# The order of the RWKV scan's instructions on TensorE: from a scheduler's order to a fixed one, with a chunk's small products together and the dense work in one block per chunk

## The chip, the cores and the metric

The kernel runs on one core of a Trainium2 chip. The metric is the device time of one execution in microseconds (us). Three executions of the kernel before took 1273.61, 1274.02 and 1277.94 us; the median is 1274.02 us.

## The reference, cut to what matters

The model is a trunk of four sub-layers on 512 positions of width 1024: a spatial-gating MLP, a ConvFFN, an RWKV-7 time mixer, a second ConvFFN, and a last RMSNorm. All of it is float32. The change touches the time mixer only:

```python
def rwkv7_mixer(h, mu, w_r, w_k, w_v, w_o, ...):
    xx = token_shift(h) - h
    xr, xw, xk, xv, xa, xg = (h + xx * mu[n] for n in range(6))
    r, k, v = xr @ w_r, xk @ w_k, xv @ w_v
    w = -softplus(-(w0 + tanh(xw @ w1) @ w2)) - 0.5
    a = sigmoid(a0 + (xa @ a1) @ a2)
    g = sigmoid(xg @ g1) @ g2
    ...
    # per head of 64: S_t = S_{t-1} diag(w_t) + (S_{t-1} a_t) b_t^T + v_t k_t^T ; y_t = S_t r_t
    y = wkv7_scan(r_h, decay, k_h, v_h, -kk, kk * a_h)
    y = group_norm(y) * ln_w + ln_b
    y = y + sum(r_h * k_h * r_k, -1) * v_h        # the bonus
    return (y * g) @ w_o
```

## The kernel before, in words

**Dense products.** A float32 product is made of three products in the format fp32r: `mm3` (L317, L318, L319) multiplies the high part of the weight with the high and the low part of the activation, and the low part of the weight with the high part of the activation. Activations lie transposed, 128 channels on the partitions and 512 positions along the row, so one such matmul is 128x128 by 128x512. They are most of the kernel's work on TensorE (PE).

**The scan.** The recurrence is computed in chunks of 64 positions: two groups of eight heads (four pairs of two heads) times eight chunks, so 16 chunks one after the other. Within a group a chunk needs the state that the chunk before leaves. In plain words a chunk does this, where each product is eight small float32 matmuls (four pairs times two heads) that a profile shows as x16, because a float32 matmul is run in two passes:

- L1194 writes the PSUM tile `us` from the state tile `vu` and the chunk's operand `st`. VectorE (DVE) copies it to `wt` (L1196). L1198 begins the outputs, PSUM tile `e`, from the same two operands.
- L1207 multiplies `wt` with the inverse `ti` into the other half of `us`. DVE copies one half of the heads into `vu` (L1208), ScalarE (ACT) copies the other half (L1209). In the program ACT's copy waits for DVE's, since both write one tile.
- L1216 multiplies `vu` with `bt` into `us`; DVE adds the decayed state `s0`, which GpSimd (POOL) made in L1203, and so writes the next chunk's `vu` (L1219, two instructions). The last chunk of a group has no such step.
- L1221 adds the second part of the outputs to `e` with 64x64 matmuls; ACT copies `e` into the tile `y` (L1224, two instructions).

So a chunk has two round trips between PE and the other engines: L1194, L1196, L1207, and L1207, L1208, L1209, L1216; and a third one through L1219 to the next chunk's L1194.

**After every second chunk** `finish` normalizes `y`: ACT squares it (L1237), DVE sums the squares (L1240), DVE and POOL raise them to the power -0.5 (L369, L370), DVE multiplies (L1243), PE transposes four times (L1247), DVE multiplies and adds (L1250). In the second group `gate` (dense products, L1104 the last of them) follows after every fourth chunk.

**What else PE does meanwhile.** The dense work of the phase is a generator, `fill`: the projections (with `value`, whose small transposes are L829 and whose bonus is L844), the gates' first product (`gates`, with weights of 128 and of 32 columns), and the output projection (`project`). The inverse of the second group's 64x64 triangles is a generator too (`invert(1)`): 31 steps of two instructions on DVE, and then 32x32 matmuls on PE, in 8 lots of 16 (L1030 and L1033).

**What sets the order.** The program is written in the order of the calls, but the framework's scheduler places each engine's instructions by its own estimate of when each is ready. Before, `weave` advances the generator `scan(g)` by a third of a chunk at a time, and after each third issues dense steps at a rate (RATES) and side steps at another, tied to an instruction already written by `issue_after`; the scheduler then mixes them. The loads of the chunks' operands (L1147 for `st`) are issued one chunk ahead on the DMA queue of SyncE (SP); three buffers hold `st`.

**Arrays.** [...] In this stretch there are dense matmuls (128x128 weights), 128x64 ones (L1194, L1198, L1216), 64x64 ones (L1207, L1221), and 32x32 ones (L1030, L1033). "Array mode" below means that shape.

Of the kernel before, what the change touches and what calls it, by code (L numbers as in the profile page):

```python
# [12 lines left out]
F32 = mybir.dt.float32  # L13
# [131 lines left out]
class Emit:  # L145
    def __init__(self, ctx, tc, A, out):
# [37 lines left out]
        self.wq = nc.scalar  # L184
        self.ktiles = 2
        self.x = []

# [112 lines left out]
    def gate_parts(self):  # L300

        t = [self.wp.tile([P, 1024], F32, tag="w32", bufs=2, name=self.uid("w32")) for _ in range(2)]
        for i in range(2):
            self.wq.dma_start(t[i], self.gd[:, i, 0:1024])
        return (1024, [tuple(x.bitcast(F32R) for x in t)]), (512, [self.pair(self.gd[:, :, 1024:], 256)])

# [6 lines left out]
    def mm3(self, acc, w, x, first, last):  # L313

        mm = self.nc.tensor.matmul
        (wh, wl), (xh, xl) = w, x
        mm(acc, wh, xh, start=first, stop=False)  # L317
        mm(acc, wh, xl, start=False, stop=False)  # L318
        mm(acc, wl, xh, start=False, stop=last)  # L319
# [412 lines left out]
    def rwkv_main(self, r, ctx, gain):  # L732
# [90 lines left out]
        def value(m, v):  # L823
# [18 lines left out]
            S.activation(wb, self.c("bones", P), AF.Copy, scale=self.p("r_k", m))  # L842
            q = self.acc("mm")
            nc.tensor.matmul(q, wb, rt[g][:, i, :], start=True, stop=True)  # L844
# [216 lines left out]
        def gates():  # L1061


            ws = ga["parts"]
            accs = [self.acc("mm")[0:n] for n in (P, 32)]
            for k in range(KT):
                x = gx[k]
                if k + 2 < KT:
                    gx.append(gate_mix(k + 2))
                for a, w, n in zip(accs, ws, (P, 32)):  # L1070
                    self.mm3(a, self.wcols(w, k * n, n), x, k == 0, k == KT - 1)
                next(tail[0], None)
                if k >= 3:
                    back(k - 3)
                yield
            for k in range(KT - 3, KT):
                back(k)
            for i, a in enumerate(accs):
                t = scratch("sq")[0:(P, 32)[i]]
                S.activation(t, a, AF.Tanh, scale=0.5)  # L1080
                V.tensor_scalar(t, t, 0.5, 0.5, ALU.mult, ALU.add)
# [83 lines left out]

        left, two = [], []

        def scan(g, late=iter(())):

            ih = [(i, hd) for i in range(4) for hd in range(2)]  # L1170
            y = None

            for c in range(NCH):
                last = c == NCH - 1
# [13 lines left out]

                def pt(i, hd):
                    o = RW * (1 - hd)  # L1190
                    return st[i][H[hd], o:o + C]

                for i, hd in ih:
# [6 lines left out]
                if not last:  # L1200
                    s0 = tile_([P, 4, C], "wt", 4)
                    for hd in range(2):
                        G.tensor_tensor(s0[H[hd]], vu[H[hd], hd], bc(gc[H[hd], 4 * g:4 * g + 4, c], C), ALU.mult)  # L1203
                self.step(late)
                yield
                for i, hd in ih:
                    nc.tensor.matmul(us[H[hd], 1, i, :], ti[g][H[hd], i, c, :], wt[H[hd], i, :], start=True, stop=True)  # L1207
                V.tensor_copy(vu[h0, 0], us[h0, 1])  # L1208
                S.copy(vu[h1, 1], us[h1, 1])  # L1209
                self.step(late)  # L1210
                if g == 1 and c == 0:
                    self.step(late)
                yield
                if not last:
# [3 lines left out]
                    for hd in range(2):  # L1218
                        V.tensor_tensor(nvu[H[hd], hd], us[H[hd], 0], s0[H[hd]], ALU.add)  # L1219
                for i, hd in ih:  # L1220
                    nc.tensor.matmul(e[H[hd], 0, i, :], pt(i, hd), vu[H[hd], hd, i, :],  # L1221
                                     start=False, stop=True, skip_group_check=True)
                for hd in range(2):
                    S.copy(y[H[c % 2], :, hd, :], e[H[hd], 0])  # L1224
                self.step(late)
                yield
                if c % 2 == 1:
                    yield from late
                    late = finish(g, c // 2, y)
            left.append(late)  # L1230

        def finish(g, b, y):
# [4 lines left out]
            S.activation(sq, y3, AF.Square)  # L1237
            yield
            ss, rs = tmp("gs", 2, 8), tmp("gr", 2, 8)
            V.tensor_reduce(ss, sq, AX.X, ALU.add)  # L1240
            self.rsqrt(ep, rs, ss, 1.0 / C, GN_EPS)
            yield
            V.tensor_tensor(y3, y3, bc(rs, C), ALU.mult)  # L1243
            yield
            q = self.acc("aux")
# [7 lines left out]
            if g == 1 and b % 2 == 1:  # L1253
                yield
                while 1 not in gw:
                    next(fill)
                for i in range(4):
                    gate(1, i, slice((b - 1) * P, (b + 1) * P))
                    if i % 2 == 1 and b == 1:
                        yield  # L1260
                if b == 3:
                    gated.add(g)
            yield

# [44 lines left out]
        for _ in inv:  # L1309
            next(fill)  # L1310
            self.step(ahead, (mybir.EngineType.PE,))
        ctx.close()
# [82 lines left out]
```

## Time and profile before

| | |
|---|---|
| median of three executions | 1274.02 us (1273.61 to 1277.94) |
| the profiled execution: its time, its span | 1274.33 us, 1272.5 us |
| mean granted clock of PE | 0.994 |
| PE busy | 1254.8 us, 99% of the span |
| DVE, ACT, POOL busy | 856.5, 629.6, 98.0 us |
| share of PE in the chain that ended last | 90% |
| the scan: first L1194, last L1104 | 737.9 us, 874.1 us |

The span is what the records of the profiled execution cover; its own time holds 1.8 us more. Times inside the execution are counted from the start of the span. A line number is that of the kernel before unless the text says otherwise. In the timelines, x16 is a run of sixteen records of one shape, and the brackets say for how long the engine was idle before it and which instruction it waited for.

### The profile page before, as it was taken

The numbers are of one execution on the slowest core, as the hardware profiler recorded it, in microseconds if no ns is written. First come the engines' busy times: TensorE is split into PE (matmuls) and PEld (weight loads), VectorE is DVE, ScalarE is ACT, GpSimd is POOL, SyncE is SP. The second block draws the span as 40 slices with busy tenths as digits, with TensorE's granted clock in tenths as the row PEclk, the third lists the DMA queues.
The fourth block names the chain that finished last, engine by engine and source line by source line (L and its number), as shares of the span: only waits on it lengthen the run. The fifth ranks groups of instructions, "written<-read, shape, count | busy, mean of one in ns | idle before, by whom it ended". The sixth has DMA issues, their size and how long they took to land.

```text
span 1272.5 us, 19534 instructions
## 1 busy us (share of the span) xinstructions
PE 1254.8 (99%) x7591; PEld 1014.3 (80%) x7591; DVE 856.5 (67%) x1403; ACT 629.6 (49%) x1082; POOL 98.0 (8%) x119
## 2 busy tenths in 40 slices
PE   9999999999999999999999999999999999999997
PEld 6878888888888888887777776677888888888886
DVE  6466568888886444675789887665677777772233
ACT  5534446555555333475686647423544444443232
POOL 4100200000000000000000022222100000000002
PEclk9999999999999999999999999999999999999999
DMA  7332357887556775335878698763233332233332
GB/s 251 108 99 83 123 173 239 244 255 240 198 169 209 216 231 161 105 106 182 220 203 226 202 245 206 203 181 133 83 99 100 100 99 91 94 94 106 93 91 79
DMA packets 115452, 201.65 MB, mean 158 GB/s; under 512 B 21600, under 2 KB 53600, under 8 KB 115360
## 3 DMA queue, kind: packets, MB, share of 16 engines
q10 hardware_dynamic: 39104, 112.87, 29.4%
q1 hardware_dynamic: 76256, 87.54, 23.1%
q8 instruction: 59, 0.97, 0.3%
q14 instruction: 33, 0.27, 0.1%
HBM read 152.93 MB, written 47.45 MB: 157 GB/s over the span
## 4 chain that ended last, share of the span: by engine, by line
PE 90%; DVE 4%; issue 1%; DMA 0%; POOL 0%; ACT 0%; DVEq 0%; ACTq 0%; POOLq 0%
PE mm L317 10%; PE mm L319 9%; PE mm L318 9%; PE aux L317 6%; PE aux L319 6%; PE aux L318 6%; PE e L318 6%; PE e L317 6%; PE e L319 6%; PE us L319 5%; PE us L318 5%; PE us L317 5%; PE aux L935 1%; PE aux L949 1%; PE us L1194 1%; PE e L1221 1%
## 5 line engine op out<-in xcount | busy, mean ns | idle before, releaser
L236 ACT CAST w<-w 128x512 fp32r<-128x512 f32 x340 | 206.8, 611 | 364.6 <-PE aux L319 91.8
L237 DVE TENSOR_TENSOR w<-w,w 128x512 fp32r<-128x512 f32 x340 | 232.1, 685 | 185.2 <-ACT w L236 184.7
L317 PE MATMUL mm<-mxh,w 128*128 128x512 f32 (+1 forms) x416 | 170.5, 410 | 0.0
L318 PE MATMUL mm<-mxl,w 128*128 128x512 f32 (+1 forms) x416 | 164.6, 396 | 0.0
L319 PE MATMUL mm<-mxh,w 128*128 128x512 f32 (+1 forms) x416 | 164.3, 395 | 0.0
L344 POOL TENSOR_TENSOR ss<-ss,sq 128x512 f32<-128x512 f32 x30 | 40.6, 1353 | 771.1 <-issue 592.9
L317 PEld LDWEIGHTS mm<-mxh,w 128*128 128x128 f32 (+1 forms) x416 | 77.6, 187 | 20.0 <-issue 3.3
L319 PEld LDWEIGHTS mm<-mxh,w 128*128 128x128 f32 (+1 forms) x416 | 77.8, 187 | 17.4 <-issue 0.7
L318 PEld LDWEIGHTS mm<-mxl,w 128*128 128x128 f32 (+1 forms) x416 | 77.9, 187 | 16.1 <-issue 1.3
L542 ACT ACTIVATE cv<-z,par 128x512 f32<-128x512 f32 x88 | 71.7, 817 | 28.1 <-DVE z L540 23.1
L317 PE MATMUL aux<-mxh,w 128*128 128x512 f32 x216 | 84.5, 391 | 0.0
L319 PE MATMUL aux<-mxh,w 128*128 128x512 f32 x216 | 84.2, 390 | 0.3 <-DVE w L237 0.3
L317 PE MATMUL us<-mxh,w 128*128 128x512 f32 x216 | 84.5, 391 | 0.0
L318 PE MATMUL aux<-mxl,w 128*128 128x512 f32 x216 | 84.1, 389 | 0.0
L318 PE MATMUL us<-mxl,w 128*128 128x512 f32 x216 | 84.1, 389 | 0.0
L319 PE MATMUL us<-mxh,w 128*128 128x512 f32 x216 | 84.0, 389 | 0.0
L317 PE MATMUL e<-mxh,w 128*128 128x512 f32 x208 | 81.4, 391 | 0.1
L318 PE MATMUL e<-mxl,w 128*128 128x512 f32 x208 | 81.1, 390 | 0.1
L319 PE MATMUL e<-mxh,w 128*128 128x512 f32 x208 | 80.9, 389 | 0.0
L543 DVE SCALAR_TENSOR_TENSOR cv<-z,par,cv 128x512 f32<-128x512 f32 x88 | 66.1, 752 | 20.0 <-ACT cv L542 20.0
L544 DVE SCALAR_TENSOR_TENSOR cv<-z,par,cv 128x512 f32<-128x512 f32 x88 | 66.0, 752 | 2.9
L319 PEld LDWEIGHTS aux<-mxh,w 128*128 128x128 f32 x216 | 40.5, 187 | 9.2 <-DVE w L237 0.8
(1088 smaller groups left out, 2599.0 us busy)
## 6 DMA issues: line engine op xcount, KB each, us to landing
w<-in_wup ACTq DMA_DIRECT2D x88, 512.0 KB, 3.7
w<-in_wdn ACTq DMA_DIRECT2D x32, 512.0 KB, 3.6
st<-std SPq DMA_DIRECT2D x30, 320.0 KB, 6.1
w<-wkd ACTq DMA_DIRECT2D x16, 512.0 KB, 4.8
w<-wvd ACTq DMA_DIRECT2D x16, 512.0 KB, 5.6
w<-wod ACTq DMA_DIRECT2D x16, 512.0 KB, 4.3
w<-in_wdn ACTq DMA_DIRECT2D x16, 384.0 KB, 3.3
w<-in_wsu ACTq DMA_DIRECT2D x8, 512.0 KB, 3.8
```

The source lines that it names most:

```text
L236: nc.scalar.copy(hi[r, :n], src)
L237: (lo_eng or nc.vector).tensor_tensor(lo[r, :n], src, hi[r, :n].bitcast(F32), ALU.subtract)
L317: mm(acc, wh, xh, start=first, stop=False)
L318: mm(acc, wh, xl, start=False, stop=False)
L319: mm(acc, wl, xh, start=False, stop=last)
L344: nc.gpsimd.tensor_tensor(self.ss, self.ss, self.sq, ALU.add)
L542: nc.scalar.activation(c, z[:, 2:], AF.Identity, scale=cw(2, i), bias=self.p("conv_b", l * 44 + i))
L543: nc.vector.scalar_tensor_tensor(c, z[:, 1:T + 1], cw(1, i), c, ALU.mult, ALU.add)
L544: nc.vector.scalar_tensor_tensor(c, z[:, 0:T], cw(0, i), c, ALU.mult, ALU.add)
L935: nc.tensor.matmul(qs[hd][:, c - ch.start, :], bk[H[hd], c, C * hd:C * hd + P], ar[H[hd], c, :], start=True, stop=True)
L949: nc.tensor.matmul(qs[hd][:, c, :], bk[H[hd], c, C * hd:C * hd + P], dg[H[hd], c, :], start=True, stop=True)
L1194: nc.tensor.matmul(us[H[hd], 0, i, :], ar(i, hd, 0), vu[:, hd, i, :], start=True, stop=True)
```

## The change

`scan(0)`, `scan(1)` and the two `weave` calls are replaced by one generator-free loop, `recurrence`, over all 16 chunks, in a section in which PE's instructions stand in the order in which they are written (the other engines' order is still the scheduler's). A chunk is written as: L1235 and L1239 (both 128x64; L1194 and L1198 before), a step of `finish`; L1252 (64x64; L1207 before), the copies to `vu` (L1253, L1254), and then, in the same array mode, the second part of the outputs of the chunk before (`outputs`, L1184; L1221 before) with their copies; L1262 (128x64; L1216 before) and the additions (L1265); those parts of `finish` that need dense matmuls; the 32x32 products of the inverse in the chunks 5, 6 and 7 of the first group (2, 3 and 3 lots); and then one block of dense work, `pump`, of 2.1 us by a count of columns (9 to 12 matmuls). So there is one place per chunk for dense work.

Three smaller edits come with it. `invert(1)` takes up to seven steps for each step of `invert(0)`, which leaves every instruction ahead of the scan where it was. The gates' 32 weight columns are run as 128, the rest zero, which takes a memset of two tiles on POOL (L309). The last value's bonus product takes a PSUM buffer of another tag.

The four listings below are the order of a built program, with no time in it; after the line and the operation stand output and inputs by name (the number behind a name tells buffers apart) and the weights' or the rows' shape.

The first is PE before, from the middle of chunk 3 of the first group to the start of chunk 4, where `e_6839` holds chunk 3's outputs and `us_6945`, `e_6946` belong to chunk 4:

```order
L1221 MATMUL e_6839<-vu_6742,st_6738 64x64
L829 MATMUL mm_6982<-cst,v_6903 128x128 x3
L1216 MATMUL us_6838<-vu_6742,cbt_6741 64x64 x8
L1221 MATMUL e_6839<-vu_6742,st_6738 64x64 x7
L829 MATMUL mm_6982<-cst,v_6903 128x128
L317 MATMUL mm_6905<-mxh_5515,w_1094_6701 128x512
L1194 MATMUL us_6945<-vu_6742,st_6834 64x64
L1198 MATMUL e_6946<-vu_6742,st_6834 64x64
L318 MATMUL mm_6905<-mxl_5516,w_1094_6701 128x512
L1194 MATMUL us_6945<-vu_6742,st_6834 64x64 x7
L1198 MATMUL e_6946<-vu_6742,st_6834 64x64 x7
L1247 MATMUL aux_6968<-cst,y_6656 128x128 x4
```

The second is PE after, for the same stretch of the program: the whole of chunk 3, whose tiles are `us_6978` and `e_6979`, while `e_6856` holds the outputs of chunk 2:

```order
L1235 MATMUL us_6978<-vu_6777,st_6851 64x64 x8
L1239 MATMUL e_6979<-vu_6777,st_6851 64x64 x8
L1252 MATMUL us_6978<-wt_6988,ti_4860 64x64 x8
L1184 MATMUL e_6856<-vu_6777,st_6773 64x64 x8
L1262 MATMUL us_6978<-vu_6777,cbt_6776 64x64 x8
L1291 MATMUL aux_7040<-cst,y_6682 128x128 x4
L323 MATMUL mm_6929<-mxh_5515,w_1094_6737 128x512
L324 MATMUL mm_6929<-mxl_5516,w_1094_6737 128x512
L325 MATMUL mm_6929<-mxh_5515,w_1094_6737 128x512
```

Before, single heads of a product stand ahead of the other seven with dense matmuls between; after, forty small matmuls of a chunk stand together and nothing dense lies between them. From the scan's first small matmul to the last gate the array mode changes 150 times before and 68 times after; the runs of dense matmuls between small ones go from 63 to 19, the changes from one small mode to another from 24 to 30.

The third listing is DVE before, around the normalization of chunks 2 and 3 (`y_6837`, `gs_7125`) in the first group:

```order
L1208 COPY vu_6941<-us_7074 64x256
L1240 TENSOR_REDUCE gs_7125<-ysq_7097 128x8
L1018 STREAM_TRANSPOSE li_7138<-tt_6617 128x32x32
L369 TENSOR_SCALAR rs_7128<-gs_7125 128x8
L1055 SCALAR_TENSOR_TENSOR sq_7156<-h_68,omu,sq_7156 128x512
L1219 TENSOR_TENSOR vu_6941<-us_7074,wt_7094 64x256 x2
L1243 TENSOR_TENSOR y_6837<-y_6837,gr_7126 128x512
L237 TENSOR_TENSOR mxl_7160<-sq_7156,mxh_7159 128x512
L1196 COPY wt_7227<-us_7217 128x256
```

The fourth is DVE after, around the same normalization (`y_6854`, `gs_7140`):

```order
L1265 TENSOR_TENSOR vu_6974<-us_7075,wt_7095 64x256 x2
L1284 TENSOR_REDUCE gs_7140<-ysq_7122 128x8
L1237 COPY wt_7173<-us_7163 128x256
L375 TENSOR_SCALAR rs_7143<-gs_7140 128x8
L1287 TENSOR_TENSOR y_6854<-y_6854,gr_7141 128x512
L1253 COPY vu_6974<-us_7163 64x256
L1265 TENSOR_TENSOR vu_7159<-us_7163,wt_7183 64x256 x2
L1294 SCALAR_TENSOR_TENSOR rt_4349<-aux_7217,par,rt_4349 128x128 x4
```

The multiplication of `y`, which waits for POOL's power, stood behind the additions (L1219) before; after, it stands between the copy to `wt` (L1237) and the copy to `vu` (L1253) of a chunk. It does so in seven chunks; in two of them the DVE part of the power (L375) stands behind the copy to `wt` as well, in the other five ahead of it.

The diff, cut to its core:

```diff
+AHEAD, SUBST, PRODUCTS, PUMP = 7, 5, (0, 0, 0, 0, 0, 2, 3, 3), (2.1, 2.1)
...
+        w = self.pair(self.gd[:, :, 1024:], 256)
+        for x in w:
+            self.nc.gpsimd.memset(x[:, 256:384].bitcast(F32), 0.0)
...
+        self.work += 3 * (acc.shape[-1] + 32) / 2400
         mm(acc, wh, xh, start=first, stop=False)
...
-            accs = [self.acc("mm")[0:n] for n in (P, 32)]
+            accs = [self.acc("mm") for _ in range(2)]
...
-                    self.mm3(a, self.wcols(w, k * n, n), x, k == 0, k == KT - 1)
+                    self.mm3(a, self.wcols(w, k * n, P), x, k == 0, k == KT - 1)
...
+        def outputs():
+            if not pend:
+                return
+            g, c, st, vu, e, y = pend.pop()
+            for i, hd in heads():
+                o = RW * (1 - hd)
+                nc.tensor.matmul(e[H[hd], 0, i, :], st[i][H[hd], o:o + C], vu[H[hd], hd, i, :],
+                                 start=False, stop=True, skip_group_check=True)
+            for hd in range(2):
+                S.copy(y[H[c % 2], :, hd, :], e[H[hd], 0])
+            if c % 2 == 1:
+                lates.append([finish(g, c // 2, y), False])
+
+        def slot(dense):
+            for late in list(lates):
+                if late[1] and not dense:
+                    continue
+                ...
+                    more = next(late[0], None)
+                ...
+
+        def pump(us):
+            self.owed += us
+            while self.owed > 0:
+                before = self.work
+                if next(fill, self) is self:
+                    return
+                self.owed -= max(self.work - before, 0.1)
+
+        def recurrence(side):
...
+            for g, c in itertools.product(range(2), range(NCH)):
...
-                self.step(late)
-                yield
+                slot(False)
+                if g == 0 and c < SUBST:
+                    self.step(side)
...
+                outputs()
+                pend.append((g, c, st, vu, e, y))
+                slot(False)
...
-                for i, hd in ih:
-                    nc.tensor.matmul(e[H[hd], 0, i, :], pt(i, hd), vu[H[hd], hd, i, :],
-                                     start=False, stop=True, skip_group_check=True)
-                for hd in range(2):
-                    S.copy(y[H[c % 2], :, hd, :], e[H[hd], 0])
...
+                slot(True)
+                if g == 0:
+                    for _ in range(PRODUCTS[c]):
+                        self.step(side)
+                pump(PUMP[g])
+            outputs()
+            while lates:
+                pump(PUMP[g])
+                slot(True)
...
-        self.weave(scan(0), inv, fill, *RATES[2], ktiles=STEPS[2])
-        for _ in inv:
-            pass
-        self.weave(scan(1, left.pop()), None, fill, *RATES[3], ktiles=STEPS[3])
-        self.weave(left.pop(), None, fill, *RATES[4], ktiles=STEPS[4])
+        self.ktiles, self.work, self.owed = 1, 0.0, 0.0
+        with tc.manual_schedule(engines={mybir.EngineType.PE}):
+            recurrence(inv)
```

More of the change, by code (lines that the diff above doesn't have):

```diff
@@ L185, in __init__ @@
         self.ktiles = 2
+        self.work = 0.0
         self.x = []
@@ L842, in value @@
             S.activation(wb, self.c("bones", P), AF.Copy, scale=self.p("r_k", m))
-            q = self.acc("mm")
+            q = self.acc("aux" if m == KT - 1 else "mm")
             nc.tensor.matmul(q, wb, rt[g][:, i, :], start=True, stop=True)
@@ L1164, in load, with heads @@
             chunks[g, c] = st, bt, vu
-        left, two = [], []
-        def scan(g, late=iter(())):
-            ih = [(i, hd) for i in range(4) for hd in range(2)]
+        two, pend, lates = [], [], []
+        def heads():
+            return [(i, hd) for i in range(4) for hd in range(2)]
+        def outputs():
[14 more added lines that the diff above has]
+                    continue
+                with ExitStack() as ctx:
+                    for eng in (mybir.EngineType.PE, mybir.EngineType.DVE):
+                        ctx.enter_context(tc.issue_after(self.last(eng)))
+                    more = next(late[0], None)
+                if more is None:
+                    lates.remove(late)
+                else:
+                    late[1] = more
+        def pump(us):
[6 more added lines that the diff above has]
+        def recurrence(side):
+            ih = heads()
             y = None
-            for c in range(NCH):
+            for g, c in itertools.product(range(2), range(NCH)):
                 last = c == NCH - 1
@@ L1203, in scan @@
                         G.tensor_tensor(s0[H[hd]], vu[H[hd], hd], bc(gc[H[hd], 4 * g:4 * g + 4, c], C), ALU.mult)
-                self.step(late)
-                yield
+                slot(False)
+                if g == 0 and c < SUBST:
+                    self.step(side)
+                if g == 1 and c == 0:
+                    for _ in side:
+                        pass
                 for i, hd in ih:
@@ L1209, in scan @@
                 S.copy(vu[h1, 1], us[h1, 1])
[L1210 to L1213, printed above, removed]
+                outputs()
+                pend.append((g, c, st, vu, e, y))
+                slot(False)
+                if g == 0 and c < SUBST:
+                    self.step(side)
                 if not last:
@@ L1219, in scan @@
                         V.tensor_tensor(nvu[H[hd], hd], us[H[hd], 0], s0[H[hd]], ALU.add)
-                for i, hd in ih:
-                    nc.tensor.matmul(e[H[hd], 0, i, :], pt(i, hd), vu[H[hd], hd, i, :],
-                                     start=False, stop=True, skip_group_check=True)
-                for hd in range(2):
-                    S.copy(y[H[c % 2], :, hd, :], e[H[hd], 0])
[L1225 to L1230, printed above, removed]
+                slot(True)
+                if g == 0:
+                    for _ in range(PRODUCTS[c]):
+                        self.step(side)
+                pump(PUMP[g])
[3 more added lines that the diff above has]
+                slot(True)
         def finish(g, b, y):
@@ L1310, in rwkv_main @@
             next(fill)
-            self.step(ahead, (mybir.EngineType.PE,))
+            for _ in range(AHEAD):
+                self.step(ahead, (mybir.EngineType.PE,))
         ctx.close()
```

18 lines of the change are left out of this document (7 added, 11 removed).

## The prediction

> **What bounds the kernel now.** I read the page first, for the engine that the time hangs on: the span, the busy times, the shares of the chain that ended last.
>
> ```profile
> span 1272.5 us, 19534 instructions
> PE 1254.8 (99%) x7591; PEld 1014.3 (80%) x7591; DVE 856.5 (67%) x1403; ACT 629.6 (49%) x1082; POOL 98.0 (8%) x119
> PE 90%; DVE 4%; issue 1%; DMA 0%; POOL 0%; ACT 0%; DVEq 0%; ACTq 0%; POOLq 0%
> ```
>
> PE is the bound. It is the same set of matmuls after the change, so time can come only from what PE spends between them: waits, and time lost when small and dense matmuls alternate. The orders differ only in the scan, 737.9 to 874.1 us; outside it nothing moves. So I read the scan next, first by windows (us, then busy time of PE, PEld, DVE, ACT, POOL, the granted clock, the DMA share, GB/s), then PE's waits in it (total, times, longest).
>
> ```profile
> 790.00:810.00 20.00, 18.66 (x352) 13.12 (x352) 11.18 (x25) 10.65 (x21) 4.88 (x4) 1.00 0.70 195
> 810.00:830.00 20.00, 17.63 (x242) 12.78 (x241) 16.50 (x36) 10.51 (x21) 5.97 (x7) 1.00 0.94 237
> ```
>
> ```profile
> PE aux L1033 <- issue: 1.3, 1, 1.3
> ...
> PE aux L318 <- DVE sg L1084: 0.2, 1, 0.2
> ```
>
> PE has six lines of waits in the whole scan (1.3, 1.2, 0.9, 0.8, 0.5 and 0.2 us), 4.9 us together: before, dense work filled every round trip to the other engines. What the filling cost shows in PE's timeline, here two chunks of the second group (start, duration, and x16 for a whole small product):
>
> ```profile
> 849.32 0.69 PE L1194 MATMUL us<-vu,st 128*64 128x64 f32 x16
> 849.84 0.64 PE L1198 MATMUL e<-vu,st 128*64 128x64 f32 x16
> 850.40 0.50 PE L317 MATMUL mm<-mxh,w 128*128 128x512 f32 x1
> ...
> 851.99 0.68 PE L1207 MATMUL us<-wt,ti 64*64 64x64 f32 x16
> 852.61 0.50 PE L317 MATMUL mm<-mxh,w 128*128 128x512 f32 x1
> ...
> 855.85 0.33 PE L1194 MATMUL us<-vu,st 128*64 128x64 f32 x2
> 856.01 0.28 PE L1198 MATMUL e<-vu,st 128*64 128x64 f32 x2
> 856.22 0.50 PE L318 MATMUL mm<-mxl,w 128*128 128x512 f32 x1
> 856.65 0.62 PE L1194 MATMUL us<-vu,st 128*64 128x64 f32 x13
> ...
> 857.73 0.66 PE L1247 MATMUL aux<-cst,y 128*128 128x128 f32 x4
> ```
>
> Matmuls overlap, so I price by start to next start. Then dense ones, among them with 32-column weights:
>
> ```profile
> 794.52 0.40 PE L319 MATMUL mm<-mxh,w 128*128 128x512 f32 x1
> 794.75 0.40 PE L317 MATMUL mm<-mxh,w 128*32 128x512 f32 x1
> 794.99 0.40 PE L318 MATMUL mm<-mxl,w 128*32 128x512 f32 x1
> ```
>
> A dense matmul followed by a dense one takes 0.23 us.
>
> **What goes.** *Dense islands.* From 850.40 to 851.99 stand six dense matmuls: 1.59 us, where six take 6 x 0.23 = 1.38, so 0.21 more. A small product takes 0.52 when one of its own mode follows (849.32 to 849.84) and 0.62 when dense work does (851.99 to 852.61), so a change behind it costs about 0.09. An island costs 0.30. There are 63 runs of dense matmuls before and 19 after: 44 x 0.30 = 13.2 us go. Six changes more between small modes, at 0.09, give 0.5 back: **-12.7**.
>
> The 32 columns that are padded to 128 give nothing: 0.23 and 0.24 us at the change of width, the same as without one. [...]
>
> *Split heads.* Before, one head of a product often ran ahead by itself.
>
> ```profile
> 836.96 0.33 PE L1221 MATMUL e<-vu,st 64*64 64x64 f32 x2
> 837.21 0.51 PE L317 MATMUL mm<-mxh,w 128*128 128x512 f32 x1
> ```
>
> The two pairs at 855.85 take 0.37 (to 856.22), and the remaining 28 passes from 856.65 to 857.73 take 1.08, no less than a full 32 (849.32 to 850.40, 1.08). So a split L1194 and L1198 costs 0.37, a split L1221 0.25. The order has 7 and 10 such: 7 x 0.37 + 10 x 0.25 = 5.1, less 17 x 0.09 that the islands' price already holds: **-3.6**.
>
> *Waits.* The six lines above are of places that no longer stand so: **-4.9**. What is late in their place comes next.
>
> **What comes.** With no dense work between a chunk's products, each round trip is covered by small products alone. Its lengths are in the timelines of DVE, ACT and POOL around the same chunk:
>
> ```profile
> 850.05 0.42 DVE L1196 COPY wt<-us 128x256 f32<-128x256 f32 x1
> 852.79 0.42 DVE L1208 COPY vu<-us 64x256 f32<-64x256 f32 x1 [2.31 <-PE us L1207]
> 853.13 0.67 DVE L1240 TENSOR_REDUCE gs<-ysq 128x8 f32<-128x512 f32 x1
> 853.84 0.17 DVE L369 TENSOR_SCALAR rs<-gs 128x8 f32<-128x8 f32 x1
> ...
> 854.99 0.88 DVE L1219 TENSOR_TENSOR vu<-us,wt 64x256 f32<-64x256 f32 x2
> 855.90 0.69 DVE L1243 TENSOR_TENSOR y<-y,gr 128x512 f32<-128x512 f32 x1
> ```
>
> ```profile
> 853.29 0.37 ACT L1209 COPY vu<-us 64x256 f32<-64x256 f32 x1 [4.36 <-DVE vu L1208]
> ```
>
> ```profile
> 854.15 1.63 POOL L370 TENSOR_TENSOR gr<-rs,mhalf 128x8 f32<-128x8 f32 x1 [6.04 <-DVE rs L369]
> ```
>
> *First trip.* L1194 starts at 849.32, DVE's copy at 850.05 (0.73 later), takes 0.42, and 0.1 passes until the next engine starts (852.79 + 0.42 to 853.29 is 0.08): 1.25 us. L1194 and L1198 cover 1.08. The wait is 0.17, sixteen times: **+2.7**.
>
> *Second trip.* L1207 starts at 851.99, DVE's copy 0.80 later, 0.42; ACT's copy, which waits for DVE's, 0.08 and 0.37; 0.1 to PE: 1.77 us. It is covered by L1252's own 0.52 (its mode stays) and the outputs of the chunk before, 0.61: the wait is 0.64 in 13 chunks, and 1.77 - 0.61 = 1.16 in the first, which has no outputs to run. Two chunks have no L1262. 13 x 0.64 + 1.16 = **+9.5**.
>
> *Third trip.* From L1262 it takes 0.80 + 0.88 + 0.1 = 1.8 us, and the dense block of 2.1 us covers it: nothing. Where the dense work ran out, it would be 1.2 us a chunk.
>
> *DVE comes late.* PE now stands still while DVE does something else first. In seven chunks the multiplication of `y` stands ahead of the copy to `vu`, and it waits for POOL. In two of them POOL can't begin before the copy to `wt` is done: 0.17 + 0.14 + 1.63 + 0.12 + 0.69 = 2.75 us (853.84 to 856.59 in the rows above), where the copy to `vu` would start 0.1 + 0.80 = 0.9 behind: 1.85 late, 3.7 for both. In the other five POOL has the dense block to finish in: between 0 and the same 1.85; I take a third, 0.6 each, 3.0. In three more chunks one other DVE instruction stands ahead of the copy to `wt`, about 0.45 us late, 1.3 together: **+8.0**, between 3.7 (the two alone) and 14.3 (all seven in full, and the 1.3). Behind the waiting instruction stands all of PE's scan, since PE runs in order.
>
> *Issue.* PE waited 1.3 + 0.5 us for its own instructions, both times in a run of 32x32 products. These now stand in lots of 32 and 48 matmuls together, so I take it as coming back: **+1.8**, between 0 and 5.
>
> *Small things.* A few transposes and gates behind `finish` still wait for DVE where they did (0.8 and 0.9 above): **+1.0**, between 0 and 2. The memset on POOL stands ahead of a product (L1244) that the end of its chunk needs only; nothing. The operand `st` is held until the next chunk's outputs:
>
> ```profile
> st<-std SPq DMA_DIRECT2D x30, 320.0 KB, 6.1
> ```
>
> The load took 6.1 us and is issued as soon as its buffer is free, now about half way through the chunk before the one before it is needed: one and a half chunks of (874.1 - 737.9) / 16 = 8.5 us, more than 6.1. Nothing, unless the queue stands.
>
> **The sum.** -12.7 - 3.6 - 4.9 + 2.7 + 9.5 + 8.0 + 1.8 + 1.0 = +1.8 us on the profiled execution's 1274.33 us, which stands 0.3 above the median of 1274.02: 1276.1 there, **1275.8** as a median. A measurement of this kernel can tell about 0.5% from no change, 6.4 us: below 1267.6 is faster, above 1280.4 slower. The forecast is no change: what PE saves by fewer mode changes it spends waiting for two copies per chunk.
>
> **The rivals.** *Faster.* The copies are late in the two chunks alone (3.7 instead of 8.0), the issue waits stay away, and an island costs a change on either side, 0.21 + 2 x 0.09 = 0.39, so that 44 x 0.09 = 4.0 more go: 1.8 - 4.3 - 1.8 - 4.0 = -8.3, **1265.7**. For it speaks that DVE is busy only 11.2 of 20 us between 790 and 810, so little else stands ahead of a copy; against it that L1198 at 849.84, with an island behind it, takes 0.56 and not 0.62 until the next start, so the higher price of an island does not hold everywhere.
>
> *Slower.* POOL's power decides the copy to `vu` in every one of the seven chunks, 14.3 instead of 8.0, and POOL's own work slows DVE's next step, as here:
>
> ```profile
> 824.77 1.10 DVE L1243 TENSOR_TENSOR y<-y,gr 128x512 f32<-128x512 f32 x1 [0.85 <-POOL gr L370]
> ```
>
> ```profile
> 824.71 1.65 POOL L1203 TENSOR_TENSOR wt<-vu,gc 64x256 f32<-64x256 f32 x2
> ```
>
> The same multiplication took 1.10 beside POOL's product and 0.69 alone: 0.41 x 7 = 2.9. That makes 1.8 + 6.3 + 2.9 = +11.0, **1285.0**. It decides the sign from the point at which DVE's lateness passes 8.0 + 4.6 = 12.6 us. For it: POOL's 1.63 us is longer than any cover but the dense block. Against it: in five of the seven chunks POOL has that block.
>
> *The clock.* The granted clock was 1.00 in both windows above, in which PE stood still for 1.3 and 2.4 us of 20, so short waits did not lower it here. The change makes some 30 short waits. If they lowered the clock to one half in the 16 dense blocks of 2.1 us, that is +34 us, **1308**. [...]
>
> *The change does not do what it says.* PE's order is fixed by the program, and the listing shows it; only the dense blocks could be shorter than 2.1 us, if weights come late.
>
> **How the numbers follow.** The forecast's case has 0.66; faster 0.15; slower 0.16; the clock 0.02; late loads or weights 0.01. The forecast's own range comes from its bounds (lateness 4 to 11, issue 0 to 5): 1270 to 1282. The range for 8 in 10 reaches to about the faster rival and takes in the near side of the slower: **1266 to 1283**. Chances: faster 0.15 x 0.7 + 0.66 x 0.06 = 0.15; slower 0.16 x 0.9 + 0.03 + 0.66 x 0.06 = 0.21; the rest, 0.64, no change.
>
> **What would show it.** In the profile after: PE's waits in the scan grow from 4.9 to about 25 us and lie on L1252 (for DVE's L1237) and on L1262 (for ACT's L1254); some 0.2 and 0.6 us each, with two or more of 2 us on L1262 or L1252 where `y` waited for POOL. PE's busy time falls by some 20 us. A clock below 1.00 in the scan, waits on L1262 mostly below 0.3, or waits on a DMA would prove steps of this wrong.

## The result and the profile after

The changed kernel takes 1284.57 us (median of five executions, 1282.88 to 1289.17) against 1274.02 us before: 10.5 us slower, ratio 1.0083 with a 95% interval of 1.0054 to 1.0113. The forecast was 1275.8 us, and its range ended at 1283. The profiled execution took 1284.10 us, 9.8 more than the one of before. A second measurement of the same kernel gave the ratio 1.0071 (1.0051 to 1.0091) from five executions; a sixth of it took 2072.93 us at a mean clock of 0.553 and is left out of every figure here.

The page of the changed kernel shows a PE that is busy for 9 us less, in a span that is 9.8 us longer:

```profile
span 1282.3 us, 19548 instructions
PE 1245.7 (97%) x7591; PEld 1016.1 (79%) x7591; DVE 855.3 (67%) x1403; ACT 629.3 (49%) x1082; POOL 98.2 (8%) x121
...
PEclk9999999999999999999999898899999999999999
```

The last line is the granted clock in 40 slices; it is below 9 three times in the scan. Before, it never was:

```profile
PEclk9999999999999999999999999999999999999999
```

These are PE's waits in the scan (total, times, longest), where before there were six lines with 4.9 us:

```profile
PE us L1262 <- ACT vu L1254: 14.4, 13, 2.8
PE us L1252 <- DVE wt L1237: 3.6, 6, 2.0
PE us L1235 <- DVE vu L1265: 1.1, 1, 1.1
PE us L1262 <- ACT rb L1254: 1.0, 1, 1.0
PE aux L1291 <- DVE rt L1112: 0.9, 1, 0.9
PE aux L323 <- DVE rt L1294: 0.7, 1, 0.7
PE aux L1039 <- DVE rt L1294: 0.6, 1, 0.6
PE mm L323 <- ACT vt L840: 0.3, 1, 0.3
PE aux L1039 <- issue: 0.2, 1, 0.2
PE mm L850 <- ACT vt L840: 0.2, 1, 0.2
```

They add up to 23.0 us. The forecast put 2.7 + 9.5 + 8.0 + 1.8 + 1.0 = 23.0 there. So the waits came as forecast in their sum, and something else is slower. The windows of the same stretches as before show it in the last columns but two, the granted clock:

```profile
790.00:810.00 20.00, 17.40 (x441) 14.39 (x440) 12.06 (x25) 12.71 (x25) 3.89 (x5) 1.00 0.69 189
810.00:830.00 20.00, 16.15 (x222) 12.83 (x221) 12.80 (x28) 8.06 (x17) 5.38 (x6) 0.83 0.69 170
```

The trace's record of the clock has three stretches at 0.50 in the scan, called falls below: 6.83 us from 781.25, 6.83 us from 815.38, 3.41 us from 842.69. Each begins in a long wait or at most 1.5 us behind its end: 2.21 us ahead of L1262 in chunk 5 of the first group, 2.83 us ahead of L1262 in chunk 1 of the second, 1.98 us ahead of L1252 in chunk 4 of the second. PE's timeline at the second one:

```profile
813.39 0.63 PE L1184 MATMUL e<-vu,st 64*64 64x64 f32 x16
816.86 1.12 PE L1262 MATMUL us<-vu,cbt 128*64 128x64 f32 x16 [2.83 <-ACT vu L1254]
817.91 1.12 PE L1291 MATMUL aux<-cst,y 128*128 128x128 f32 x4
818.68 0.78 PE L323 MATMUL mm<-mxh,w 128*128 128x512 f32 x1
819.25 0.63 PE L324 MATMUL mm<-mxl,w 128*128 128x512 f32 x1
819.68 0.63 PE L325 MATMUL mm<-mxh,w 128*128 128x512 f32 x1
```

A small product that takes 0.62 us takes 1.05 here (816.86 to 817.91), and dense matmuls follow each other after 0.43 us and not 0.23. DVE's timeline says why PE waited so long:

```profile
812.40 0.42 DVE L1237 COPY wt<-us 128x256 f32<-128x256 f32 x1
813.89 1.10 DVE L1287 TENSOR_TENSOR y<-y,gr 128x512 f32<-128x512 f32 x1 [1.07 <-POOL gr L376]
814.91 1.11 DVE L239 TENSOR_TENSOR mxl<-sq,mxh 128x512 fp32r<-128x512 f32 x1
815.94 0.41 DVE L1253 COPY vu<-us 64x256 f32<-64x256 f32 x1
```

Between the copies to `wt` and to `vu` stand the multiplication of `y`, which waits for POOL, and another one for the gates, both slowed to 1.1 us (0.69 in the rows of other chunks and runs).

### The profile page after: what moved, and what is told of

The parts are those of the page before. It is cut to its first block, busy times and chain, and to the rows that moved or that the text cites. A ratio compares the mean times of both kernels' runs of the same rounds, so it can differ in the third digit from the quotient of the medians.

```text
span 1282.3 us, 19548 instructions
## 1 busy us (share of the span) xinstructions
PE 1245.7 (97%) x7591; PEld 1016.1 (79%) x7591; DVE 855.3 (67%) x1403; ACT 629.3 (49%) x1082; POOL 98.2 (8%) x121
## 5 line engine op out<-in xcount | busy, mean ns | idle before, releaser
L323 PE MATMUL mm<-mxh,w 128*128 128x512 f32 x416 | 172.4, 414 | 0.3 <-ACT vt L840 0.3
L324 PE MATMUL mm<-mxl,w 128*128 128x512 f32 x416 | 165.0, 397 | 0.0
L325 PE MATMUL mm<-mxh,w 128*128 128x512 f32 x416 | 164.8, 396 | 0.0
L323 PEld LDWEIGHTS mm<-mxh,w 128*128 128x128 f32 x416 | 79.4, 191 | 21.3 <-issue 3.8
L325 PEld LDWEIGHTS mm<-mxh,w 128*128 128x128 f32 x416 | 79.3, 191 | 17.4 <-issue 0.7
L324 PEld LDWEIGHTS mm<-mxl,w 128*128 128x128 f32 x416 | 79.6, 191 | 16.3 <-issue 1.8
```

## The experiments

The account that they test: the change saves work on PE, adds 18 us of waits (23.0 - 4.9), and adds three falls of the clock. Theory A says that the falls are a cost of their own, up to half of their 17.1 us. Theory B says that they cost nothing, since PE waits anyway, and that the change saved less than was forecast. Theories C, D and E are about why PE waits. The changed kernel was run again and eleven variants of it were run, each timed against the kernel before on the same chip. The last two columns have PE's waits and the time at half clock between 680 and 905 us; they are of one profiled execution each. The mean clock is given over all executions, the lowest and the highest, since the falls differ from one execution to the next (for the kernel before, over the 45 executions that stand beside the others').

| kernel | median us | ratio (95%) | mean clock | waits us | half clock us |
|---|---|---|---|---|---|
| before | 1274.02 | | 0.990 to 0.997 | 5.4 | 6.8 |
| changed | 1284.57 | 1.0083 (1.0054 to 1.0113) | 0.984 to 0.990 | 23.5 | 23.9 |
| changed, again | 1284.18 | 1.0071 (1.0051 to 1.0091) | 0.985 to 0.992 | 25.9 | 17.1 |
| filler that itself waits | 1289.13 | 1.0121 (1.0101 to 1.0141) | 0.987 to 0.993 | 25.5 | 23.9 |
| filler, long waits | 1280.65 | 1.0058 (1.0038 to 1.0077) | 0.992 to 0.995 | 15.7 | 10.2 |
| filler, all waits | 1280.74 | 1.0041 (1.0026 to 1.0057) | 0.992 to 0.996 | 11.7 | 10.2 |
| y behind | 1283.83 | 1.0078 (1.0064 to 1.0092) | 0.987 to 0.990 | 25.2 | 20.5 |
| DVE in written order | 1299.62 | 1.0201 (1.0181 to 1.0221) | 0.979 to 0.982 | 32.3 | 44.4 |
| the same, block in two | 1301.17 | 1.0211 (1.0187 to 1.0236) | 0.976 to 0.984 | 29.8 | 47.8 |
| outputs in their own chunk | 1294.18 | 1.0163 (1.0143 to 1.0183) | 0.983 to 0.987 | 27.4 | 27.3 |
| block in two | 1281.07 | 1.0065 (1.0051 to 1.0079) | 0.986 to 0.989 | 19.3 | 17.1 |
| block in two, y behind | 1279.20 | 1.0049 (1.0036 to 1.0063) | 0.987 to 0.991 | 18.2 | 20.5 |
| the same, last transposes later | 1273.01 | 0.9982 (0.9966 to 0.9997) | 0.990 to 0.997 | 16.2 | 3.4 |
| block in three, y behind, last transposes later | 1270.95 | 0.9974 (0.9960 to 0.9987) | 0.991 to 0.995 | 12.7 | 3.4 |

**A filler that waits itself.** The first try to keep PE active in the three long waits:

```diff
+        FILL = {(0, 5, 2): 3, (1, 1, 2): 4, (1, 4, 1): 3}
+        def filler(key, q):
+            for _ in range(FILL.get(key, 0)):
+                nc.tensor.matmul(q, self.cst[:, 0:P], self.cst[:, 0:256], start=True, stop=True, ...)
...
+                filler((g, c, 1), us[:, 1])     # ahead of L1252
+                filler((g, c, 2), us[:, 0])     # ahead of L1262
```

> The changed kernel, with ten matmuls (128x128 by 128x256, float32) that compute nothing that is used, written into a PSUM half that the next product overwrites: three ahead of L1262 in chunk 5 of the first group, four ahead of L1262 in chunk 1 of the second, three ahead of L1252 in chunk 4 of the second. These are PE's three waits after which the granted clock fell to 0.50 (for 6.8, 6.8 and 3.4 us); the other engines' order stays. Theory A (the low clock costs what it stretches, half of 17 us): PE is active in the waits, the clock stays at 1.00, the waits end at the same time, and the kernel takes 8.5 us less, about 1276. Theory B (the low clock falls into waits and on work that had slack; the waits alone made the change slow): no change, 1284 to 1286.

It told nothing of the theories. The filler's output lies in the PSUM tile that ACT reads, so the filler took over the wait:

```profile
PE us L1271 <- ACT vu L1262: 10.0, 11, 1.9
PE us L1218 <- ACT vu L1262: 5.0, 2, 2.8
PE us L1218 <- DVE wt L1244: 2.0, 1, 2.0
```

L1218 is the filler, and it added work behind the waits instead of in them: 1289.13 us.

**A filler without a wait.** The same with `e[:, 1]`, which nobody reads, as its output, and

```diff
+        FILL = {(0, 0, 2): 2, (0, 3, 2): 2, (0, 4, 2): 2, (0, 5, 2): 4, (1, 1, 2): 5, (1, 3, 2): 3, (1, 4, 1): 3}
```

> The changed kernel, with matmuls that compute nothing that is used (128x128 by 128x256, float32, about 0.49 us each), written without a wait into the unused half of the chunk's PSUM tile e, ahead of the products that waited longest: 2, 2, 2 and 4 ahead of L1262 in chunks 0, 3, 4 and 5 of the first group, 5 and 3 in chunks 1 and 3 of the second, 3 ahead of L1252 in chunk 4 of the second. Each lot is shorter than the wait it stands in; the other engines' order stays. So PE does no more useful work and the chunks take as long, but PE is active. Theory A (a low clock follows stretches of 3.4 us in which PE is little active, and costs half of its length): the three falls in the scan go, 8.5 us less, about 1276. Theory B (the low clock costs nothing here, the waits alone made the change slow): no change, 1284 to 1286.

PE's timeline at chunk 1 of the second group shows the filler in the place of the wait, of which 0.48 us are left:

```profile
814.40 0.63 PE L1184 MATMUL e<-vu,st 64*64 64x64 f32 x16
814.97 2.42 PE L1218 MATMUL e<-cst 128*128 128x256 f32 x10
817.87 0.69 PE L1271 MATMUL us<-vu,cbt 128*64 128x64 f32 x16 [0.48 <-ACT vu L1262]
```

The three falls are gone; one of 3.41 us came elsewhere (750.7). The mean granted clock of its six executions is 0.992 to 0.995, against 0.984 to 0.990 for the changed kernel. The time is 1280.65, where A expected 1276 and B 1284 or more. From one chunk's first L1235 to the next's, chunk 1 of the second group takes 9.5 us instead of 11.9, chunk 4 takes 7.7 instead of 9.1. But chunk 1 of the first group, with the new fall, takes 8.4 instead of 6.0; 0.9 of these 2.4 us are a longer wait ahead of the same product (1.65 instead of 0.75), and 1.5 are the fall's. So these falls are a cost, each less than half of its length: 2.4 us for one of 6.83, 1.4 and 1.5 for those of 3.41. PE stands still in part of a fall; of the 6.83 us from 815.38 it is busy for 5.35.

**The changed kernel again, and a filler in all waits.** The second has one filler more in each chunk whose wait on L1262 was 0.54 to 0.75 us:

```diff
+        FILL = {(0, 0, 2): 2, (0, 1, 2): 1, (0, 2, 2): 1, (0, 3, 2): 2, (0, 4, 2): 2, (0, 5, 2): 4, (0, 6, 2): 1, (1, 0, 2): 1,
+                (1, 1, 2): 5, (1, 2, 2): 1, (1, 3, 2): 3, (1, 4, 1): 3, (1, 4, 2): 1, (1, 5, 2): 1, (1, 6, 2): 1}
```

> The changed kernel once more, for a comparison on the same chip with the two kernels below: 1283 to 1289 us, with falls of the clock in the scan that need not stand in the same chunks.

> As the first kernel whose useless matmuls stood in the long waits without a wait of their own, and one such matmul (0.49 us) more in each chunk whose wait on L1262 was 0.54 to 0.75 us. The waits that PE is seen to make shrink to some 6 us, the chunks take as long but for mode changes of some 0.1 to 0.2 us at the small ones. Theory A: no fall of the clock in the scan; per fall of 3.4 us at half clock 1.2 to 1.7 us go, against the changed kernel on the same chip 5 to 8 us less, less 2 for the added changes of mode. Theory B: 0 to 2 us more than the changed kernel.

On the same chip the ratios are 1.0071 and 1.0041: 3.8 us less with the filler, at the lower end of A's 3 to 6, and not B's 0 to 2 us more. The intervals overlap slightly (1.0051 to 1.0091, 1.0026 to 1.0057). One fall of 6.83 us still came in the profiled execution, at 800.2, where A had none. Useless work made the kernel faster, but not as fast as the kernel before: at nearly that kernel's clock it still takes 0.4% longer, so the clock is one part of the loss and not all of it. The rerun of the changed kernel shows more. In chunk 5 of the first group it has the same wait as the first time, 2.21 us, but no fall:

```profile
775.59 0.63 PE L1184 MATMUL e<-vu,st 64*64 64x64 f32 x16
778.43 0.69 PE L1262 MATMUL us<-vu,cbt 128*64 128x64 f32 x16 [2.21 <-ACT vu L1254]
```

The chunk takes 13.2 us instead of 15.5, so that fall of 6.83 us cost 2.3. In its place this execution has a fall of 3.41 us at 801.2, and chunk 7 takes 11.5 us instead of 8.9, with 1.1 of that in a longer wait (1.3 us for PE's own instructions). In the first profile of the changed kernel the beginnings of the falls lie 34.13 us (815.38 - 781.25) and 27.31 us (842.69 - 815.38) apart, ten and eight times the 3.41 us of the shortest fall. The windows of 3.41 us that end where a fall begins, in the same profile, with one window that was not followed by a fall ahead of them:

```profile
760.77:764.18 3.41, 1.76 (x46) 1.55 (x42) 3.27 (x9) 1.73 (x4) 1.01 (x2) 1.00 0.67 166
777.84:781.25 3.41, 1.35 (x29) 1.12 (x30) 1.55 (x4) 2.23 (x5) 0.56 (x2) 1.00 0.68 173
811.97:815.38 3.41, 1.66 (x50) 1.38 (x46) 2.31 (x4) 1.35 (x3) 3.33 (x3) 1.00 0.65 119
839.28:842.69 3.41, 1.16 (x34) 1.01 (x32) 2.29 (x5) 0.75 (x2) 0.00 (x0) 1.00 0.21 61
```

And in the rerun, counted back in steps of 3.41 us from its fall at 801.2, around the same wait of chunk 5:

```profile
773.89:777.30 3.41, 2.28 (x62) 2.01 (x62) 1.54 (x4) 2.98 (x4) 2.49 (x3) 1.00 0.01 3
777.30:780.72 3.42, 2.29 (x84) 2.05 (x84) 2.06 (x7) 2.14 (x4) 0.93 (x2) 1.00 0.85 205
```

Before a fall PE was busy for 1.35, 1.66 and 1.16 of 3.41 us; where it was 1.76 nothing fell. In the rerun the border of two windows cuts the wait in two, both windows hold 2.3 us of work, and the clock was 1.00 in both. One program thus has different falls in different executions, and its times go with its mean clock: 1288.74 and 1289.17 us at 0.984, 1282.88 and 1284.57 at 0.990. The kernel before does the same, from 1271.00 at 0.997 to 1279.92 at 0.990.

That gives a second price for the clock, out of all executions and not of single chunks. Call (1 - mean clock) x time the missing clock: it is 7.3 us on average in the 45 executions of the kernel before, and 15.7 in the ten of the changed one. A straight line through the times, with one slope for both kernels, rises by 0.76 us (standard error 0.05) for each microsecond of it, and the changed kernel lies 4.4 us (0.6) higher at the same clock. So of the 10.8 us between the two averages about 6.3 go with the clock and 4.4 do not.

**`y` behind the copy to `vu`.**

```diff
                         G.tensor_tensor(s0[H[hd]], vu[H[hd], hd], ...)
-                slot(False)
                 if g == 0 and c < SUBST:
```

> The changed kernel without the step of finish between L1239 and L1252, so that on DVE the multiplication of y stands behind the copy to vu and no longer ahead of it. The part of the waits on L1262 that goes beyond 0.56 us should go in five chunks: (1.65 + 1.11 + 2.21 + 2.83 + 1.91) - 5 x 0.56 = 6.9 us. Theory A: two of the three falls of the clock go with them, 6.8 us more; about 1271. Theory B: 1284.6 - 6.9, about 1278.

1283.83 us: no difference that can be told, neither A's 1271 nor B's 1278. The waits did not fall, 25.2 us. In chunk 1 of the second group PE still waits 2.40 us, and DVE's timeline shows the next in the queue:

```profile
813.12 0.42 DVE L1237 COPY wt<-us 128x256 f32<-128x256 f32 x1
813.77 0.69 DVE L239 TENSOR_TENSOR mxl<-sq,mxh 128x512 fp32r<-128x512 f32 x1 [0.23 <-ACT mxh L238]
815.19 0.42 DVE L1252 COPY vu<-us 64x256 f32<-64x256 f32 x1 [0.73 <-POOL wt L1244]
```

`mxl` of the gates and POOL's product (L1244, which reads the tile that the copy writes) keep the copy back in the place of `y`. Taking one of three late things away gave nothing.

**DVE in written order too.** The inverse's steps and `y` go behind the copies, and DVE gets PE's treatment:

```diff
-                slot(False)
-                if g == 0 and c < SUBST:
-                    self.step(side)
...
-                    for _ in range(PRODUCTS[c]):
+                    for _ in range(PRODUCTS[c] + (c < SUBST)):
...
-        with tc.manual_schedule(engines={mybir.EngineType.PE}):
+        with tc.manual_schedule(engines={mybir.EngineType.PE, mybir.EngineType.DVE}):
```

> The changed kernel with DVE's instructions, too, in the order in which they are written, the multiplication of y behind the copy to vu, and the inverse's DVE steps behind that copy and behind the additions: nothing stands any more between a chunk's copies to wt and to vu. Theory C (the waits beyond the trips' own length come from the order in which the scheduler put DVE's other work): waits of PE in the scan fall from 22.7 to about 12 (16 x 0.17, 14 x 0.56 and 1.5), the clock falls once or twice less, and the kernel takes about 1267. Theory D (they come from trips that are as long in any order): as e_y_behind, 1284.

> As e_dve, and one dense step (three matmuls) of the chunk's block ahead of L1262. Theory C: the second round trip is covered as well; waits about 4 us, no fall of the clock in the scan, 14 islands more at 0.2 to 0.3: about 1260, faster than the kernel before. Theory D: as e_both, 1279.

The second one adds the dense step of the next experiment. Both are the slowest of all, 1299.62 and 1301.17 us, and theory C fell in this form. PE's waits moved from the copy to `vu` to the copy to `wt`:

```profile
PE us L1249 <- DVE wt L1237: 17.6, 11, 3.7
PE us L1259 <- ACT vu L1251: 6.5, 13, 0.6
```

In written order the DVE work of a whole dense block stands ahead of the next chunk's copy to `wt`. The copy to `vu` is now prompt, 0.6 us at most, but the wait has only changed its place, up to 3.7 us of it at once, and between 680 and 905 us the clock is at one half for 44.4 us.

**The block of dense work in two.**

```diff
                 if not last:
+                    before = self.work
+                    next(fill, None)
+                    self.owed -= self.work - before
                     for i, hd in ih:
                         nc.tensor.matmul(us[H[hd], 0, i, :], bt[:, i, hd, :], ...)
```

> The changed kernel with one dense step (three matmuls, 0.7 us) of the chunk's block moved between the outputs and L1262, so that it covers the second round trip. The waits on L1262 fall from 15.4 to about 5.6 us, and 14 islands more cost 0.30 each, 4.2. Theory A: the clock falls once or not at all, about 5 us more go: 1274. Theory B, in which an island is worth half as much: 1284.6 - 9.8 + 2.1, about 1277.

> Both edits together: y behind the copy to vu, and one dense step ahead of L1262. Waits on L1262 nearly gone (15.4 us), 14 more islands. Theory A: 1284.6 - 15.4 + 4.2 - 6.8 (at least two falls of the clock less), about 1266.5, faster than the kernel before. Theory B: 1284.6 - 15.4 + 2.1, about 1271, about as fast as the kernel before.

Alone it gave 1281.07 us, with `y` behind as well 1279.20: less than theory A's gains and less than B's. Of the changed kernel's 23.5 us of waits the expectations took away 9.8 and 15.4; 19.3 and 18.2 us were left. The line of the second trip did fall as expected with the block in two alone, from 15.4 to 4.1 us, but others grew: the first trip's from 3.6 to 6.2, the third's from 1.1 to 2.9, and one of 2.8 came. With both edits the second trip still waits 3.4 us, the first 5.8, and at the end of the first group PE waits 2.79 us for `y` ahead of the transposes. The window of 3.41 us with this wait is the emptiest of this run's scan, and a fall of 6.83 us follows:

```profile
793.35:796.76 3.41, 0.62 (x8) 0.48 (x10) 1.14 (x2) 1.10 (x3) 3.05 (x3) 1.00 0.66 142
796.76:803.59 6.83, 6.58 (x106) 5.61 (x106) 3.61 (x8) 4.88 (x8) 0.00 (x0) 0.50 0.78 230
```

The next experiment moves those transposes behind the chunk's dense work, in a group's last chunk alone:

```diff
-                slot(True)
+                if not last:
+                    slot(True)
...
                 pump(PUMP[g])
+                if last:
+                    slot(True)
```

> The kernel with both edits (y behind the copy to vu, one dense step ahead of L1262), and the transposes of a group's last chunk behind its dense work, where PE waited 2.8 us for y and the clock then fell for 6.8 us. By theory A 2.8 + 2 to 3.4 less than 1279.2: 1273 to 1275. If the fall comes anyway: 1276.5.

1273.01 us, 6.2 less, where A had 4.8 to 6.2 and a fall that comes anyway would have left 1276.5. Waits fell by 2.0 us, and the time at half clock by 17.1 in the two profiled executions. That is more than usual: the new kernel's profile is of its second fastest execution, 1270.83 us at a clock of 0.996. Over all executions the missing clock fell from 13.3 us on average to 9.6, which at 0.76 is 2.8 us. So the clock and the waits both have a part in what was gained, and the shares aren't settled.

**The block in three.** With a dense step ahead of L1252 as well, so that each of the chunk's three round trips has some dense work in it:

```diff
+        def dense():
+            before = self.work
+            next(fill, None)
+            self.owed -= self.work - before
...
+                dense()        # ahead of L1252
...
+                    dense()    # ahead of L1262
```

> The changed kernel with its block of dense work in three parts of one step, ahead of L1252, ahead of L1262 and at the chunk's end, the multiplication of y behind the copy to vu, and the transposes of a group's last chunk behind its dense work. Theory A with the prices so far (an island 0.25, 28 islands more than the changed kernel, 7; waits from 23 to about 8 us; falls of the clock as in the kernel before, 5 us less): 1284.6 + 7 - 15 - 5 to 7, about 1270, faster than the kernel before. If the waits are of DVE's order rather than of the missing cover (theory E), they stay at about 15 us, as with two parts, and the time at 1279.

1270.95 us, the fastest of all: 0.26% below the kernel before (0.13 to 0.40%). Theory A gave 1270, E 1279. (Against the kernel with two parts the times overlap, 1269.05 to 1274.83 and 1267.83 to 1276.27.) Waits are 12.7 us, more than the 8 that A expected, and no line is long:

```profile
PE us L1240 <- DVE vu L1271: 2.9, 3, 2.1
PE us L1268 <- ACT vu L1259: 2.8, 3, 1.3
PE us L1257 <- DVE wt L1242: 2.7, 4, 1.1
PE us L1240 <- DMA vu<-vtd: 2.3, 2, 1.5
```

The clock fell once, for 3.41 us.

**The outputs in their own chunk.** The reverse of one part of the change:

```diff
-                outputs()
                 pend.append((g, c, st, vu, e, y))
...
+                outputs()
                 slot(True)
```

> The changed kernel with the second part of the outputs back in its own chunk, behind L1262, so that L1252 alone covers the second round trip: the wait on L1262 grows by the outputs' 0.52 to 0.61 us in 13 chunks, 7 to 8 us. By theory A more stretches come near the point where the clock falls, so between 8 and 13 us more: 1292 to 1298. If late outputs cover nothing that counts: 1284.6.

1294.18 us, 9.6 more than the changed kernel, inside what was expected. The late outputs are a part of the change that helps: without them the changed kernel is 20 us slower than the kernel before.

## Why the prediction was wrong

The forecast's sum for the waits was right in total, 23.0 us on both sides. That it agrees to a tenth is luck, since the terms were off by up to 1.7 us in both directions and made up for each other. The first trip was given 2.7 us; the waits of 0.17 to 0.40 us on L1252 make 1.6. The second trip was given 0.64 us; it is 0.54 to 0.57 where nothing else is late, and 1.04 in the first chunk where 1.16 stood. DVE's lateness was given 8.0 us; it is 7.1 on L1262 above 0.56 and some 1.8 on L1252, 8.9. Issue waits were 0.2 and not 1.8; the small ones were 2.7 and the one on L1235 1.1, where 1.0 stood. The slower rival had 14.3 us of DVE's lateness in all seven chunks and 2.9 of slowed steps. Its 1285.0 us is close to the measured time by luck and not by its mechanism: only four of the seven chunks were late on L1262 by more than 1 us (1.65, 2.21, 2.83, 1.91 in all), and the lateness as a whole stayed near the forecast's.

The step that failed is in the rival on the clock: "The granted clock was 1.00 in both windows above, in which PE stood still for 1.3 and 2.4 us of 20, so short waits did not lower it here." It got a chance of 0.02 and a price of 34 us for all dense blocks. The windows of 20 us were too wide to show what stood ahead of the three falls here: 3.41 us in which PE was busy for 1.16 to 1.66 us. Before, counted in the same way from that execution's own fall at 727.27, the emptiest 3.41 us in the scan are busy for 2.07 us, and the clock was 1.00:

```profile
792.13:795.54 3.41, 2.07 (x26) 1.13 (x19) 2.19 (x5) 2.64 (x6) 1.77 (x1) 1.00 1.01 301
```

The forecast saw the long waits come, "with two or more of 2 us", and did not ask what they would do to the matmuls behind them. Three falls came, worth 2.3, 2.4 and 1.4 us by the comparisons above, 6.1 together. Without them the profiled execution would have been 9.8 - 6.1 = 3.7 us slower than before, inside the forecast's own range; the line through all executions says 4.4. The forecast had named the sign, a clock below 1.00 in the scan.

What is left of the difference is the saving, which no run measured by itself. 9.8 = 23.0 - 4.9 + 6.1 - 14.4, so by this sum the islands and split heads gave 14.4 us, where 12.7 + 3.6 = 16.3 was forecast. Which of the two was priced too high was not tried apart. The forecast's other sign, PE busy for some 20 us less, came as 9.1 us: the saving is smaller, and at half clock the matmuls themselves take longer (L1262 1.12 us from 816.86, 0.69 from 779.90). The steps on the third trip, on the load of `st` and on POOL's memset held: no line of the waits names them, but for 1.1 us on L1235 where DVE's transposes of the inverse stood ahead.

## What to carry to other kernels

Grouping small matmuls saved some 14 us here, by the sum above (an estimate, since no run measured it by itself), but it took the dense work out of the round trips. Three waits of 1.98 to 2.83 us were paid twice in the changed kernel's profile, as waits and as a clock of 0.50 behind them that cost 1.4 to 2.4 us each. So look at PE's longest wait, not only at the sum: with one dense step in each round trip, `y` behind the copy and a group's last transposes later, the kernel was 13.6 us faster than with one block per chunk. And where one engine's order is fixed by hand, read the queues of the engines that it now waits for: with the first late instruction moved away the next one was late here, and PE's waits stayed (25.2 us, 23.5 in the changed kernel).

## What the runs showed of the hardware that was not expected

In the changed kernel's profile the granted clock went to 0.50 three times in the scan, for 6.83, 6.83 and 3.41 us, each time after 3.41 us with little work on PE: 1.35, 1.66 and 1.16 us. After a window with 1.76 us it stayed at 1.00. With the block in two and `y` behind, 0.62 us of 3.41 stand ahead of a fall, and with the block in three 1.28 us of 3.40 (768.30 to 771.70, the clock at 0.50 from 771.70 to 775.10).

PE's busy time is not all that goes with a fall, as the kernel before shows. Its one fall in this part, 6.83 us from 727.27, comes just ahead of the scan and after a window in which PE was busy all the time (the windows here start 0.09 us late; PE's busy time is the second number behind the window):

```profile
723.95:727.36 3.41, 3.41 (x65) 3.30 (x66) 3.35 (x4) 1.85 (x5) 0.00 (x0) 0.99 0.80 243
727.36:730.77 3.41, 3.41 (x42) 3.02 (x43) 3.00 (x11) 1.65 (x4) 0.00 (x0) 0.50 0.52 162
```

The first of these windows holds almost only small matmuls, of 64 rows (L949) and of 32x32 (L1033). Why the clock fell there no run shows.
